# A fourth summed K pair in the gate projection of a SwiGLU block, and where its forms and the 512-column rows are kept

## The chip, the cores and the metric

The kernel runs on one core of a Trainium2 chip. The metric is the device time of one execution in microseconds (us). TensorE (PE) does the matmuls, VectorE (DVE) and ScalarE (ACT) prepare operands and move results, GpSimd (POOL) does a little, and the queue of SyncE (SP) starts nearly all transfers from memory.

## The reference

One layer of an encoder on 256 tokens of width 2048, all in float32: an attention part (latent attention beside differential attention), cross attention into 256 memory tokens, and a SwiGLU block of hidden width 5632, each added to the running x, then a last normalization. The change lies in the last block:

```python
hf = rms_norm(x, g_ffn[layer])
x = x + (jax.nn.silu(hf @ w_gate[layer]) * (hf @ w_up[layer])) @ w_down[layer]
return rms_norm(x, g_final)
```

## The kernel before, in words

**Products.** Each float32 operand is split in two parts: `h`, a rounded copy made by ACT (line 103), and `l`, what is left of it, made by DVE (line 104, a subtraction that needs the ACT copy). A product is three matmuls (`mm`, lines 95 to 97): h·h, h·l and l·h. A weight is read from memory into `wraw` (1 MB, three buffers), split into `wh`/`wl` tiles of 1024 columns (four buffers of each), and then used by PE. The activations stand still in PE, the weights move through it, 512 columns at a time.

**Chunks.** The hidden columns of SwiGLU are worked in one narrow chunk of 512 columns (`narrow_chunk`) and five wide chunks of 1024 columns (`wide_chunk`). There are three groups: the narrow chunk with the first wide one, then two wide chunks, then two wide chunks. After each group its hidden columns are multiplied with `w_down` (`wide_add`) into the running x. A wide chunk is a gate projection, Silu on its result, an up projection (both `wide_result`), the product of the two, and a transposition of that.

**K pairs.** In `wide_project` the 2048 input features are taken as eight pairs of 128-row blocks. A pair with 256 tokens and 1024 output columns is a 2x2 by 2x2 block product. There are two ways to do it, written as letters in `GU_KINDS` and `DN_KINDS`:

- `P`, plain: eight block products, that is 24 matmuls of 512 columns. Its weights are two `wh`/`wl` tiles of 1024 columns.
- `W`, summed: seven block products by a Strassen-Winograd scheme, that is 21 matmuls. DVE first makes sums of weight blocks in `tsum` (line 721 over 1024 columns, lines 725 and 726 over 512 each). The splits are then three tiles of 1024 columns (`b11`, `t13`, `t24`) and one of 512 (`b21`); `t24` lies in a place of its own, `wh2`/`wl2`, which has one buffer. Three of the products go straight into the accumulators `accs`, four into PSUM tiles `Q` that all summed pairs of a projection share.

When the last summed pair is done, `leave` (lines 751 to 755) combines the four Q on DVE; when the projection is done, `join` (line 759) adds the accumulators, four DVE instructions. The eight PSUM banks are two sets of four; accumulators and Q swap sets after every projection, and the transposes of the hidden columns (lines 327 and 850) use the same tiles as the next Q.

**The activations' forms.** `normalized_pairs` makes the stationary operands once, for gate and up together. A plain pair is a split of 512 columns. A summed pair (`summed_pair`) has eight forms, namely its four blocks and four sums of them (lines 684 to 687), then split. Pairs 2, 4 and 6 are summed. Plain pairs share two tiles of four K blocks; the fifth plain pair, number 7, has tiles `oddh`/`oddl` of its own in the pool `wsum`.

**Orders.** The gate takes the pairs in the order 0 to 7, whose kinds are P P W P W P W P. The up projection takes 0, 2, 1, 4, 3, 6, 5, 7, whose kinds are P W P W P W P P.

**What sets the order of work.** Only the transfers keep the written order. For all the rest a planner, which runs the program against its own timing of each instruction, lays down a fixed sequence for each engine ahead of the run. So PE does not take the matmuls pair by pair: where an operand of one pair is not yet there, matmuls of a neighbouring pair are put in between.

**Rows of 512.** `nat` gives tiles of 128 x 512 float32 with seven buffers in a pool that lives through the whole kernel. In SwiGLU they hold the sums of `summed_pair`, `sg` and `h` of the narrow chunk, and `v` and `u` of `wide_add`. The pools of attention are closed ahead of SwiGLU (line 646), and `wsum` is opened in their space (line 647).

Of the kernel before, what the change touches and what calls it, by code (L numbers as in the profile page):

```python
# [11 lines left out]
F32 = mybir.dt.float32  # L12
F32R = mybir.dt.float32r
# [6 lines left out]
P = 128  # L20
S = 256
# [14 lines left out]
NFC = FF // 512  # L36
NPC = (FF - 512) // 1024

GU_KINDS = "PPWPWPWP"

G_ORDER, U_ORDER = (0, 1, 2, 3, 4, 5, 6, 7), (0, 2, 1, 4, 3, 6, 5, 7)

DN_KINDS = "PP" + "PPPW" * NPC

# [32 lines left out]
def encoder_block(ctx: ExitStack, tc: tile.TileContext, a, out):  # L77
# [33 lines left out]
    def act_tile(shape=(P, 4, S), name="act"):  # L111
        return Split(
            act.tile(list(shape), F32R, name=name + "_h", tag="act"),
            act.tile(list(shape), F32R, name=name + "_l", tag="act"),
        )
# [37 lines left out]
    def project(actT, pieces, before=None, fine=0):  # L153
# [13 lines left out]
                kt += 1  # L167
        return accs

    def nat(name):  # L170
        return sb.tile([P, 512], F32, name=name, tag="nat", bufs=7)


    banks = [(pacc, "acc"), (pps, "ps")]
# [81 lines left out]
    for i in range(8):  # L256
# [10 lines left out]
        for k, w in enumerate(weights(a["w_in_lat"][i], i == 0, before_k=x0T.load_one if i == 0 else None,  # L267
                                      cut=QL if i == 0 else None, raw=lat_raw if i == 0 else None)):
            xk = x0T(2 * i + k)
            for tt in range(NT):  # L270
                x = xk[:, tt * P:(tt + 1) * P]
# [373 lines left out]
    soft_pool.close()  # L645
    attention.close()
    wsum = ctx.enter_context(tc.tile_pool(name="wsum", bufs=1))


    def pair_raw(src):  # L650
# [22 lines left out]
        def at(self, k, tt):  # L673
            return self.plain[:, k, tt * P:(tt + 1) * P] if self.forms is None else self.forms[:, 2 * tt + k, :]

    def summed_pair(a0, a1, in_psum=False):

        f = act_tile((P, 8, P), name="forms")
        s = nat("sums").rearrange("p (n t) -> p n t", n=4)
        a21 = a1[:, 0, :]  # L680
        if in_psum:
            a21 = nat("a21")[:, :P]
            nc.scalar.copy(out=a21, in_=a1[:, 0, :])
        nc.vector.tensor_tensor(out=s[:, 0, :], in0=a21, in1=a1[:, 1, :], op=ALU.subtract)
        nc.vector.tensor_tensor(out=s[:, 1, :], in0=a0[:, 0, :], in1=s[:, 0, :], op=ALU.subtract)
        nc.vector.tensor_tensor(out=s[:, 2, :], in0=a0[:, 0, :], in1=a21, op=ALU.subtract)
        nc.vector.tensor_tensor(out=s[:, 3, :], in0=a0[:, 1, :], in1=s[:, 1, :], op=ALU.subtract)
        split_into(f[:, 0:2, :], a0)
        split_into(f[:, 2:4, :], a1)
        split_into(f[:, 4:8, :], s)  # L690
        return Pair(forms=f)
# [97 lines left out]
    def normalized_pairs():  # L789

        rb = nat("rb")
        rps = ps_tile("rps")
        for tt in range(NT):
            nc.vector.tensor_copy(out=rb[:, tt * P:(tt + 1) * P], in_=rstdf[:, tt:tt + 1].to_broadcast([P, P]))
            nc.tensor.transpose(out=rps[:, tt * P:(tt + 1) * P], in_=rb[:, tt * P:(tt + 1) * P], identity=ident)
        rrow = nat("rrow")
        nc.scalar.copy(out=rrow[:, :S], in_=rps[:, :S])
        for xr in x2raw:
            nc.vector.tensor_tensor(out=xr, in0=xr, in1=rrow[:, :S].unsqueeze(1).to_broadcast([P, 4, S]), op=ALU.mult)
        pairs = []  # L800
        t, n = None, 4
        for i, kind in enumerate(GU_KINDS):
            xr = x2raw[i // 2][:, i % 2 * 2:i % 2 * 2 + 2, :]
            if kind == "P":
                if n == 4 and "P" in GU_KINDS[i + 1:]:
                    t, n = act_tile(name="x2n"), 0
                elif n == 4:
                    t = Split(*[wsum.tile([P, 2, S], F32R, name="odd" + x, tag="odd" + x, bufs=1) for x in "hl"])
                    n = 0
                split_into(t[:, n:n + 2, :], xr)  # L810
                pairs.append(Pair(t[:, n:n + 2, :]))
                n += 2
            else:
                pairs.append(summed_pair(xr[:, :, :P], xr[:, :, P:]))
        return pairs

    def narrow_chunk(c):
# [13 lines left out]

    def wide_chunk(c, spare):

        g = wide_result(xn, a["w_gate"][c], G_ORDER, GU_KINDS)
        for tt in range(NT):
            for oc in range(2):
                nc.scalar.activation(g[tt][:, oc, :], g[tt][:, oc, :], AF.Silu)
        u = wide_result(xn, a["w_up"][c], U_ORDER, GU_KINDS)
        t = act_tile(name="hT")
        pts = []  # L840
        for oc in range(2):
            for tt in range(NT):
                h = u[tt][:, oc, :]
                nc.vector.tensor_tensor(out=h, in0=h, in1=g[tt][:, oc, :], op=ALU.mult)
                if oc == 0:
                    transposed(t, h, tt, 4)
                    continue
                pt = ps_tile("pt")
                for j in range(4):
                    nc.tensor.transpose(out=pt[:, j * P:(j + 1) * P], in_=h[:, j * P:(j + 1) * P], identity=ident)  # L850
                pts.append(pt.rearrange("p (j t) -> p j t", t=P))
                split_into(spare[:, :, tt * P:(tt + 1) * P], pts[tt][:, 0:2, :])
        return [Pair(t[:, 0:2, :]), Pair(t[:, 2:4, :]), Pair(spare),
                summed_pair(pts[0][:, 2:4, :], pts[1][:, 2:4, :], True)]


    fss = small.tile([P, NT, 7], F32, name="fss", tag="fss", bufs=1)
# [103 lines left out]
def _lay_out(i):  # L961
# [32 lines left out]
        "w_xo": _pieces(i["w_xo"][0]),  # L994
        "w_gate0": _pieces(i["w_gate"][0][:, :512]),
        "w_up0": _pieces(i["w_up"][0][:, :512]),
        "w_gate": _pairs(i["w_gate"][0][:, 512:], GU_KINDS),
        "w_up": _pairs(i["w_up"][0][:, 512:], GU_KINDS),
        "w_dn": _pairs(i["w_down"][0], DN_KINDS),
        "w_down": _pieces(i["w_down"][0][-2048:, 1024:]).transpose(1, 0, 2, 3, 4),  # L1000
    }
# [18 lines left out]
```

## Time and profile before

| | |
|---|---|
| median of three runs | 1149.32 us (1148.9 to 1149.41) |
| the profiled execution's own time | 1149.22 us |
| its span, first to last instruction | 1147.4 us |
| granted TensorE clock over the span | 0.998 |
| SwiGLU's wide projections | about 480 us to 1054 us of the span |

Times in the trace are microseconds from the start of the span. "Busy" of an engine is time in which it executed something; the digits of the page are tenths of a slice of the span. In the list of groups a line reads: source line, engine, operation, tile written <- tiles read, shape, count, then busy time and the mean duration in ns, then the idle time of the engine just ahead and what ended it. In a timeline a line reads: start, duration, engine, line, operation, tiles, count, and in brackets the idle time ahead of it with what ended it. A duration can be longer than the distance between two starts, because neighbouring instructions of an engine overlap; the distance is what a queue of them costs.

### The profile page before, as it was taken

The numbers are of one execution on the slowest core, as the hardware profiler recorded it, in microseconds if no ns is written. First come the engines' busy times: TensorE is split into PE (matmuls) and PEld (weight loads), VectorE is DVE, ScalarE is ACT, GpSimd is POOL, SyncE is SP. The second block draws the span as 40 slices with busy tenths as digits, with TensorE's granted clock in tenths as the row PEclk, the third lists the DMA queues.
The fourth block names the chain that finished last, engine by engine and source line by source line (L and its number), as shares of the span: only waits on it lengthen the run. The fifth ranks groups of instructions, "written<-read, shape, count | busy, mean of one in ns | idle before, by whom it ended". The sixth has DMA issues, their size and how long they took to land.

```text
span 1147.4 us, 14386 instructions
## 1 busy us (share of the span) xinstructions
PE 1138.3 (99%) x5480; PEld 955.3 (83%) x5480; DVE 931.8 (81%) x1231; ACT 628.2 (55%) x885; POOL 68.9 (6%) x81
## 2 busy tenths in 40 slices
PE   9999999999999999999999999999999999999997
PEld 7888888888888888888888888888888888888887
DVE  7698766586868776989988889998888899898873
ACT  6755454554666555665544555564544564654552
POOL 5920000001000000000000000000000000000021
PEclk9999999999999999999999999999999999999999
DMA  9555334444764445455656555555555555565551
GB/s 359 217 211 187 126 130 169 176 150 182 294 214 158 166 159 182 153 214 187 217 183 220 184 190 214 183 205 198 188 215 187 210 190 205 195 233 210 191 212 75
DMA packets 33766, 222.15 MB, mean 194 GB/s; under 512 B 4128, under 2 KB 4896, under 8 KB 8992
## 3 DMA queue, kind: packets, MB, share of 16 engines
q1 hardware_dynamic: 32256, 216.86, 52.7%
q0 software_dynamic: 864, 3.15, 0.8%
q10 hardware_dynamic: 576, 1.21, 0.3%
q8 instruction: 43, 0.70, 0.2%
q14 instruction: 27, 0.22, 0.1%
HBM read 219.11 MB, written 2.10 MB: 193 GB/s over the span
## 4 chain that ended last, share of the span: by engine, by line
PE 98%; issue 0%; DMA 0%; DVE 0%; ACT 0%; POOLq 0%; POOL 0%; DVEq 0%; ACTq 0%
PE acc L95 27%; PE acc L96 27%; PE acc L97 27%; PE q L95 3%; PE q L97 3%; PE q L96 3%; PE pt L327 2%; PE ppt L474 1%; PE psc L97 1%; PE psc L96 1%; PE psc L95 1%; PE acckv L95 0%; PE acckv L97 0%; PE acckv L96 0%; PE pt L850 0%
## 5 line engine op out<-in xcount | busy, mean ns | idle before, releaser
L103 ACT CAST wh<-wraw 128x1024 fp32r<-128x1024 f32 (+2 forms) x399 | 395.3, 1003 | 368.6 <-PE acc L97 311.9
L104 DVE TENSOR_TENSOR wl<-wraw,wh 128x1024 fp32r<-128x1024 f32 (+2 forms) x399 | 464.2, 1175 | 142.6 <-ACT wh L103 140.6
L96 PE MATMUL acc<-wl,x2n_h 128*128 128x512 f32 x320 | 124.6, 390 | 0.0
L97 PE MATMUL acc<-wh,x2n_l 128*128 128x512 f32 x320 | 123.9, 389 | 0.0
L95 PE MATMUL acc<-wh,x2n_h 128*128 128x512 f32 x320 | 107.5, 390 | 0.0
L96 PE MATMUL acc<-wl,hT_h 128*128 128x512 f32 (+1 forms) x272 | 103.3, 381 | 0.0
L97 PE MATMUL acc<-wh,hT_l 128*128 128x512 f32 (+1 forms) x272 | 102.5, 380 | 0.0
L104 DVE TENSOR_TENSOR wl<-tsum,wh 128x1024 fp32r<-128x1024 f32 x76 | 91.9, 1220 | 8.6 <-ACT wh L103 8.5
L103 ACT CAST wh<-tsum 128x1024 fp32r<-128x1024 f32 x76 | 79.0, 1052 | 32.6 <-PE acc L97 11.9
L95 PE MATMUL acc<-wh,hT_h 128*128 128x512 f32 (+1 forms) x272 | 89.3, 381 | 0.0
L96 PE MATMUL acc<-wl,x0T_h 128*128 128x512 f32 x224 | 88.1, 394 | 0.1
L97 PE MATMUL acc<-wh,x0T_l 128*128 128x512 f32 x224 | 87.8, 393 | 0.0
L95 PE MATMUL acc<-wh,x0T_h 128*128 128x512 f32 x224 | 87.3, 395 | 0.4 <-ACT x0T_h L106 0.4
L97 PEld LDWEIGHTS acc<-wh,x2n_l 128*128 128x128 f32 x320 | 60.1, 188 | 12.4
L96 PEld LDWEIGHTS acc<-wl,x2n_h 128*128 128x128 f32 x320 | 60.1, 188 | 12.3
L95 PEld LDWEIGHTS acc<-wh,x2n_h 128*128 128x128 f32 x320 | 59.9, 188 | 12.3
L97 PEld LDWEIGHTS acc<-wh,hT_l 128*128 128x128 f32 x272 | 51.2, 188 | 9.6
L96 PE MATMUL q<-wl,forms_h 128*128 128x512 f32 x152 | 59.1, 389 | 0.0
L96 PEld LDWEIGHTS acc<-wl,hT_h 128*128 128x128 f32 x272 | 51.2, 188 | 9.5
L95 PEld LDWEIGHTS acc<-wh,hT_h 128*128 128x128 f32 x272 | 51.0, 188 | 9.5
L97 PE MATMUL q<-wh,forms_l 128*128 128x512 f32 x152 | 58.8, 389 | 0.0
L95 PE MATMUL q<-wh,forms_h 128*128 128x512 f32 x152 | 53.3, 389 | 0.0
(369 smaller groups left out, 2227.1 us busy)
## 6 DMA issues: line engine op xcount, KB each, us to landing
wraw<-in_w_gate SPq DMA_DIRECT2D x44, 1024.0 KB, 4.8
wraw<-in_w_up SPq DMA_DIRECT2D x44, 1024.0 KB, 4.8
wraw<-in_w_dn SPq DMA_DIRECT2D x36, 1024.0 KB, 4.8
wraw<-in_w_in SPq DMA_DIRECT2D x24, 1024.0 KB, 4.8
wraw<-in_w_out SPq DMA_DIRECT2D x16, 1024.0 KB, 4.8
wraw<-in_w_down SPq DMA_DIRECT2D x8, 1024.0 KB, 4.8
wraw<-in_w_in_lat SPq DMA_DIRECT2D x7, 832.0 KB, 7.4
wraw<-in_w_xk SPq DMA_DIRECT2D x4, 1024.0 KB, 6.3
```

Of the source, the lines that this page charges most:

```text
L95: nc.tensor.matmul(o, l.h, r.h, start=start, stop=False)
L96: nc.tensor.matmul(o, l.h, r.l, start=False, stop=False)
L97: nc.tensor.matmul(o, l.l, r.h, start=False, stop=stop)
L103: last_cast[0] = nc.scalar.copy(out=dst.h, in_=src).ins
L104: last_split[0] = nc.vector.tensor_tensor(out=dst.l, in0=src, in1=dst.h.bitcast(F32), op=ALU.subtract).ins
L327: nc.tensor.transpose(out=pt[:, j * P:(j + 1) * P], in_=src[:, j * P:(j + 1) * P], identity=ident)
L474: nc.tensor.transpose(out=pt[:, kt * S + tt * P:kt * S + (tt + 1) * P], in_=p[:, tt, kt * P:(kt + 1) * P], identity=ident)
```

## The change

The gate gets four summed pairs, numbers 1, 3, 5 and 7. The up projection keeps three, now 1, 3 and 5; its pair 7 is plain, and takes its four blocks out of the forms that the gate's pair 7 has. The gate's order is 0, 2, 1, 3, 4, 5, 7, 6, whose kinds are P P W W P W W P. The up projection's order is 0 to 7, whose kinds are P W P W P W P P, as before. The forms of pair 7 lie in `wsum` in place of `oddh`/`oddl`. The rows of 512 move: seven buffers in attention's pool, then five in `wsum`. The weights are laid out in memory ahead of the launch by the same letters (`_pairs`), each pair still 1 MB.

```diff
-GU_KINDS = "PPWPWPWP"
-
-G_ORDER, U_ORDER = (0, 1, 2, 3, 4, 5, 6, 7), (0, 2, 1, 4, 3, 6, 5, 7)
+G_KINDS, U_KINDS = "PWPWPWPW", "PWPWPWPP"
+
+G_ORDER, U_ORDER = (0, 2, 1, 3, 4, 5, 7, 6), (0, 1, 2, 3, 4, 5, 6, 7)
...
+    nat_pool = [early, 7]
+
     def nat(name):
-        return sb.tile([P, 512], F32, name=name, tag="nat", bufs=7)
+        pool, bufs = nat_pool
+        return pool.tile([P, 512], F32, name=name, tag="nat", bufs=bufs)
...
     wsum = ctx.enter_context(tc.tile_pool(name="wsum", bufs=1))
+    nat_pool[:] = wsum, 5
...
-    def summed_pair(a0, a1, in_psum=False):
-
-        f = act_tile((P, 8, P), name="forms")
+    def summed_pair(a0, a1, f=None, in_psum=False):
+
+        f = f or act_tile((P, 8, P), name="forms")
...
-        for i, kind in enumerate(GU_KINDS):
+        for i, kind in enumerate(G_KINDS):
             xr = x2raw[i // 2][:, i % 2 * 2:i % 2 * 2 + 2, :]
             if kind == "P":
-                if n == 4 and "P" in GU_KINDS[i + 1:]:
+                if n == 4:
                     t, n = act_tile(name="x2n"), 0
-                elif n == 4:
-                    t = Split(*[wsum.tile([P, 2, S], F32R, name="odd" + x, tag="odd" + x, bufs=1) for x in "hl"])
-                    n = 0
...
             else:
-                pairs.append(summed_pair(xr[:, :, :P], xr[:, :, P:]))
+                f = None
+                if i == 7:
+                    f = Split(*[wsum.tile([P, 8, P], F32R, name="forms" + x, tag="forms" + x, bufs=1) for x in "hl"])
+                pairs.append(summed_pair(xr[:, :, :P], xr[:, :, P:], f))
...
-        g = wide_result(xn, a["w_gate"][c], G_ORDER, GU_KINDS)
+        g = wide_result(xn, a["w_gate"][c], G_ORDER, G_KINDS)
...
-        u = wide_result(xn, a["w_up"][c], U_ORDER, GU_KINDS)
+        u = wide_result(xn, a["w_up"][c], U_ORDER, U_KINDS)
```

More of the change, by code (lines that the diff above doesn't have):

```diff
@@ L853, in wide_chunk @@
         return [Pair(t[:, 0:2, :]), Pair(t[:, 2:4, :]), Pair(spare),
-                summed_pair(pts[0][:, 2:4, :], pts[1][:, 2:4, :], True)]
+                summed_pair(pts[0][:, 2:4, :], pts[1][:, 2:4, :], in_psum=True)]
     fss = small.tile([P, NT, 7], F32, name="fss", tag="fss", bufs=1)
@@ L996, in _lay_out @@
         "w_up0": _pieces(i["w_up"][0][:, :512]),
-        "w_gate": _pairs(i["w_gate"][0][:, 512:], GU_KINDS),
-        "w_up": _pairs(i["w_up"][0][:, 512:], GU_KINDS),
+        "w_gate": _pairs(i["w_gate"][0][:, 512:], G_KINDS),
+        "w_up": _pairs(i["w_up"][0][:, 512:], U_KINDS),
         "w_dn": _pairs(i["w_down"][0], DN_KINDS),
```

## Prediction

> **What bounds the kernel now.** I read the page first: busy times, the slices, the chain.
>
> ```profile
> PE 1138.3 (99%) x5480; PEld 955.3 (83%) x5480; DVE 931.8 (81%) x1231; ACT 628.2 (55%) x885; POOL 68.9 (6%) x81
> DVE  7698766586868776989988889998888899898873
> PE 98%; issue 0%; DMA 0%; DVE 0%; ACT 0%; POOLq 0%; POOL 0%; DVEq 0%; ACTq 0%
> ```
>
> PE has work nearly all the time, and the chain that ended last is 98% PE. DVE is next: 81% over the span, but eights and nines from the seventeenth slice on, where SwiGLU begins. So PE sets the time, and the engine that feeds it has little left just where the change lies. The busy time by stage shows how little:
>
> ```profile
> 487.00:530.00 43.00, 43.00 (x193) 35.62 (x192) 38.56 (x43) 26.36 (x30) 0.00 (x0) 1.00 0.54 195
> 629.00:671.00 42.00, 42.00 (x187) 34.80 (x186) 35.99 (x40) 22.72 (x24) 0.00 (x0) 1.00 0.56 198
> 714.00:757.00 43.00, 43.00 (x199) 35.68 (x198) 39.86 (x50) 24.33 (x32) 0.00 (x0) 1.00 0.52 182
> 884.00:926.00 42.00, 42.00 (x187) 34.79 (x186) 35.59 (x38) 22.30 (x25) 0.00 (x0) 1.00 0.55 195
> 968.00:1011.00 43.00, 43.00 (x199) 35.72 (x198) 39.87 (x50) 24.38 (x31) 0.00 (x0) 1.00 0.50 180
> 1011.00:1054.00 43.00, 43.00 (x192) 35.60 (x191) 39.60 (x47) 23.94 (x28) 1.10 (x2) 1.00 0.64 236
> ```
>
> The columns after the stage are its length, then PE, PEld, DVE, ACT and POOL, the granted clock, the DMA share and GB/s. The first five rows are roughly the five gate projections. PE is busy without a gap in each, at clock 1.00. DVE is idle 4.44 us in the first (43.00 - 38.56), 6.01 in the second, 3.14 in the third, 6.41 in the fourth, 3.13 in the fifth. The second and fourth are the first chunk of a group and follow a down projection; the third and fifth are the second chunk and follow an up projection, whose joins, products and transposes fall into them.
>
> **What PE saves.** A summed pair in place of a plain one is 21 matmuls for 24. The price of one is the distance between starts:
>
> ```profile
> 729.35 0.39 PE L95 MATMUL acc<-wh,x2n_h 128*128 128x512 f32 x1
> 734.11 0.39 PE L97 MATMUL acc<-wh,x2n_l 128*128 128x512 f32 x1
> ```
>
> Between these two starts lie 21 steps of PE with no wait, so a matmul costs 4.76 / 21 = 0.2267 us; the 0.39 is a length, of which more than a third overlaps the next. Three fewer are 0.68 us, in five gates 3.40 us. This is the whole gain, if PE never waits. The up projection keeps three summed pairs in the same sequence of kinds, and its pair 7 is still 24 matmuls, so nothing changes there.
>
> **What DVE gets.** These are neighbours in DVE's queue, and the two splits by shape:
>
> ```profile
> 639.93 1.22 DVE L721 TENSOR_TENSOR tsum<-wraw 128x1024 f32<-128x1024 f32 x1
> 641.18 0.69 DVE L725 TENSOR_TENSOR tsum<-tsum,wraw 128x512 f32<-128x512 f32 x1
> 641.79 1.22 DVE L104 TENSOR_TENSOR wl<-wraw,wh 128x1024 fp32r<-128x1024 f32 x1
> 642.93 0.69 DVE L726 TENSOR_TENSOR tsum<-tsum,wraw 128x512 f32<-128x512 f32 x1
> 643.53 1.22 DVE L104 TENSOR_TENSOR wl<-wraw,wh 128x1024 fp32r<-128x1024 f32 x1
> L104 DVE TENSOR_TENSOR wl<-wraw,wh 128x1024 fp32r<-128x1024 f32 x344 | 420.3, 1233 | 115.6 <-ACT wh L103 113.8
> L104 DVE TENSOR_TENSOR wl<-wraw,wh 128x512 fp32r<-128x512 f32 x39 | 26.9, 691 | 20.4 <-ACT wh L103 20.1
> ```
>
> From 641.79 to 642.93 an instruction of 1024 columns took 1.14 us of the queue, from 642.93 to 643.53 one of 512 took 0.60. A plain pair has two splits of 1024: 2.28. A summed pair has three of 1024, one of 512, an add of 1024 and two of 512: 4 x 1.14 + 3 x 0.60 = 6.36. One more summed pair is 4.08 us more of DVE in each gate. Set against its matmuls, a plain pair leaves DVE a surplus of 24 x 0.2267 - 2.28 = 3.16 us, a summed pair a deficit of 6.36 - 4.76 = 1.60, and the new order has two summed pairs in a row, twice: 3.20 of deficit each time, which the plain pair between just repays. The gate shortens by 0.68, so a gate needs 4.08 + 0.68 = 4.76 us of DVE's idle time if PE is not to wait; what is missing is PE's waiting, which gives DVE the time back.
>
> The Trainium skill (VectorE: DVE Perf Modes, "The DRAIN you can't avoid") says that the next DVE instruction does not start until the pipeline is empty. The row at 643.53 disagrees: it starts 0.60 after one that is 0.69 long. By the page the full durations would count, and the added work would be 2 x 1.22 + 3 x 0.69 = 4.51 us, an estimate.
>
> **Once, in the first gate,** DVE also makes the forms of a fourth pair in place of the split of the fifth plain one:
>
> ```profile
> L104 DVE TENSOR_TENSOR forms_l<-sums,forms_h 128x512 fp32r<-128x512 f32 x8 | 5.4, 684 | 0.0
> L104 DVE TENSOR_TENSOR forms_l<-x2T_f,forms_h 128x256 fp32r<-128x256 f32 x6 | 2.3, 419 | 0.0
> L684 DVE TENSOR_TENSOR sums<-x2T_f 128x128 f32<-128x128 f32 x3 | 0.9, 284 | 0.0
> ```
>
> The split of the sums costs what the split of the plain pair did. Left are four sums and two splits of 256; less the overlap of 0.08 or 0.09 that the queue rows show, 4 x 0.20 + 2 x 0.34 = 1.48 us. DVE has no idle time just there, so it is paid out of the first gate's.
>
> **The sum.** The need is 4.76 us per gate, in the first 4.76 + 1.48 = 6.24. But a gate need not end even: DVE's lead over PE can be smaller at its end, and the up projection after it has idle time (43.00 - 39.60 = 3.40 in the sixth row). The four weight buffers hold at most two plain pairs, 10.88 us of PE. I let the lead take up what the deficit of one summed pair is, 1.60 us, since the up projection has more than that left to rebuild it. The second and fourth gates have 6.01 and 6.41: no wait. The third lacks 4.76 - 3.14 - 1.60 = 0.02, the fifth 0.03, the first 6.24 - 4.44 - 1.60 = 0.20. That is 0.25 us if all of DVE's idle time can be used. It can not quite be, because part of it is a full buffer and not want of work:
>
> ```profile
> 502.47 1.23 DVE L721 TENSOR_TENSOR tsum<-wraw 128x1024 f32<-128x1024 f32 x1 [0.21 <-DMA wraw<-in_w_gate]
> 513.69 1.23 DVE L104 TENSOR_TENSOR wl<-wraw,wh 128x1024 fp32r<-128x1024 f32 x1 [2.37 <-ACT wh L103]
> 515.49 1.23 DVE L104 TENSOR_TENSOR wl<-wraw,wh 128x1024 fp32r<-128x1024 f32 x1 [0.57 <-ACT wh L103]
> 730.68 1.23 DVE L104 TENSOR_TENSOR wl<-wraw,wh 128x1024 fp32r<-128x1024 f32 x1 [0.40 <-ACT wh L103]
> 736.80 3.50 DVE L104 TENSOR_TENSOR wl<-wraw,wh 128x1024 fp32r<-128x1024 f32 x3 [0.63 <-ACT wh L103]
> 745.67 0.69 DVE L104 TENSOR_TENSOR wl<-wraw,wh 128x512 fp32r<-128x512 f32 x1 [0.39 <-ACT wh L103]
> 747.00 1.23 DVE L104 TENSOR_TENSOR wl<-tsum,wh 128x1024 fp32r<-128x1024 f32 x1 [0.64 <-ACT wh L103]
> ```
>
> The wait at 730.68 lies ahead of the place where the second summed pair now comes, and what DVE could do then has no buffer. I take 0.25 of such lost time in each of the three tight gates, between 0 and the 0.40 of that row, nearer to the row. PE then waits 0.25 + 0.75 = 1.0 us in all, and the gain is 3.40 - 1.0 = 2.4 us. By the page's rule on the pipeline 0.43 more would be missing in each of the three, and the gain would be 1.1.
>
> **Costed at nothing.** ACT makes one more copy of 1024 and one of 512 per gate; it is busy 22 to 26 us of 42 to 43. The transfers are the same bytes, and two summed pairs in a row ask 1 MB per 4.76 us, some 220 GB/s, where the sixth row shows 236. The rows of 512: five buffers for what a group takes in turn (two per wide chunk, two per down half) come round only after another stage. Tight is only the narrow chunk, where the second `sg` would now reuse the second `sums`:
>
> ```profile
> 480.19 0.69 DVE L104 TENSOR_TENSOR forms_l<-sums,forms_h 128x512 fp32r<-128x512 f32 x1
> 481.45 1.29 DVE L104 TENSOR_TENSOR forms_l<-sums,forms_h 128x512 fp32r<-128x512 f32 x2
> 483.79 0.75 DVE L828 SCALAR_TENSOR_TENSOR h<-acc,x2Tr,sg 128x512 f32<-128x512 f32 x1
> ```
>
> If the first split in the pair at 481.45 is the second `sums`, it ends about 482.1, so `sg` (0.69) is there at 482.8, a microsecond before `h` needs it at 483.79. Without that cover the accumulators of the first gate would come free up to 1 us late, once.
>
> **Rivals.**
>
> *DVE's idle time is of no use where it lies.* Up to the fifth pair the gate has as many summed pairs as before, and the extra one comes seventh; then only the idle time late in a gate counts. In the third gate that is 1.66 of 3.14 (the rows at 736.80, 745.67 and 747.00), in the first 3.15 of 4.44 (the rows from 502.47 on). PE waits 4.76 - 1.66 = 3.10 in the third and (taken alike) the fifth, and 6.24 - 3.15 = 3.09 in the first, 9.29 in all; the lead of 1.60 takes 4.80 of it, and 4.49 - 3.40 = 1.1 us slower is left, within what counts as no change. Without the lead it is 5.9. For it: DVE is 93% busy in these stages. Against it: the planner puts matmuls of one pair among those of another, and so far PE never waits. Chance 0.30, at 1150.4 us, from 1147.0 to 1151.6 as the lead gives back more or less. In its extreme, DVE sets the pace of whole gates, and all five pay 4.08: 20.4 + 1.5 = 21.9 slower, 1171 us. The Trainium skill (Perfetto Trace Analysis, "Identifying the Most-Contended Engine") points there: matmul busy time is not the measure of PE, the busy share of weight loads is, and that is 83% against DVE's 93%. The trace speaks against it, since DVE's own waits in these rows end with ACT copies that wait for PE's buffers. Chance 0.02.
>
> *A wait for PSUM takes the place of the filler.* In the second chunk of a group two of the first summed pair's Q tiles are the banks of the last transposes, free only when the hidden columns' forms are split:
>
> ```profile
> 722.98 0.60 PE L850 MATMUL pt<-ident,res 128*128 128x128 f32 x4
> 734.88 0.68 DVE L104 TENSOR_TENSOR forms_l<-sums,forms_h 128x512 fp32r<-128x512 f32 x1
> 735.47 0.39 PE L95 MATMUL q<-wh,forms_h 128*128 128x512 f32 x1
> ```
>
> Meanwhile PE does the plain pair that follows, the 5.44 us from 729.35. Now a summed pair follows, of which only the twelve matmuls that need neither these banks nor `wh2` can run: 2.72 us. PE would wait the other 2.72, or, with DVE's 4.08 queued ahead of those splits, up to 6.80. No row is nearer to either; the middle is 4.76. In the two gates that is 9.5, less 3.4, plus 0.2 for the first: 6.3 us slower, 1155.6 us. At the low end it is 2.2 slower, 1151.6. It decides from (2.3 + 3.4 - 0.2) / 2 = 2.75 us a gate. Against it: DVE needs only some 2 us for these forms, and the transposes are done at 723.6, so the planner can draw them forward by several us. Chance 0.20.
>
> **The numbers.** About 0.2% (2.3 us) is what a measurement here can tell from no change. The forecast, 2.4 us of gain, has 0.48: faster. On the profiled execution it is 1149.22 - 2.4 = 1146.8, on the median 1149.32 - 2.4 = 1146.9. No change has 0.30, slower 0.20 + 0.02. The low end is the full 3.40 and the 0.4 that the runs spread: 1145.5. The high end takes in the first rival and the lower part of the second: 1153.0. The forecast's own range is 1145.5 to 1147.0.
>
> **What would show it.** Right: 15 matmuls fewer, PE's busy share still 99%, the five gates some 0.5 us shorter each, DVE above 95% in the third and fifth, and waits of PE for `wl` of about 1 us in all, after the second of two summed pairs. Wrong: PE idle before `q` ended by forms (the second rival), PE idle for `wl` of 3 us or more in the gates or the first pairs of the up projections (the first), or idle in the narrow chunk ended by `sg` or `h`.

## The result, and the profile after

The change makes the kernel slower: 1157.26 us median of six runs (1157.05 to 1158.17) against 1149.36 us (1148.9 to 1149.78) for the kernel before, a ratio of 1.0069 (95% interval 1.0058 to 1.0079), so 7.9 us. The prediction was 1146.9 us with a range of 1145.5 to 1153.0. The profiled execution took 1157.05 us with a span of 1155.3 us at a granted clock of 0.998, as before.

The page of the kernel after, its busy line, DVE's digits and the chain:

```profile
PE 1140.2 (99%) x5465; PEld 951.3 (82%) x5465; DVE 953.3 (83%) x1262; ACT 633.1 (55%) x897; POOL 67.6 (6%) x81
DVE  7688766586867776999988898999888998999873
PE 94%; DVE 3%; ACT 1%; issue 1%; DMA 0%; POOLq 0%; POOL 0%; DVEq 0%; ACTq 0%
```

The 15 matmuls are gone, PE is still shown 99% busy, and its busy time has grown. That is the trap of this page: a matmul that starts late is shown with a longer duration (0.50 us in the rows below where its neighbours have 0.39), and each duration overlaps the next start anyway. What tells is the chain, which now passes through DVE and ACT, and the distance between starts. The same five stretches of time as in the prediction (length, PE, PEld, DVE, ACT, POOL, clock, DMA share, GB/s); the work in them stands a few us later than before:

```profile
487.00:530.00 43.00, 42.31 (x186) 33.94 (x185) 40.73 (x46) 25.20 (x31) 0.00 (x0) 1.00 0.53 196
629.00:671.00 42.00, 42.00 (x187) 34.78 (x186) 38.54 (x42) 22.71 (x25) 0.00 (x0) 1.00 0.53 185
714.00:757.00 43.00, 41.56 (x187) 33.15 (x187) 41.02 (x53) 26.02 (x33) 0.00 (x0) 1.00 0.46 166
884.00:926.00 42.00, 42.00 (x187) 34.78 (x186) 38.53 (x41) 23.25 (x26) 0.00 (x0) 1.00 0.53 191
968.00:1011.00 43.00, 41.57 (x187) 33.15 (x187) 41.04 (x53) 24.24 (x32) 0.00 (x0) 1.00 0.44 150
```

In the third, 187 instructions of PE start where 199 did, and DVE still has 1.98 of its 3.14 us of idle time left (43.00 - 41.02): PE lost time while the idle time that was to prevent it lay unused. The same work ends 2.7 us later than before after the first group, 5.2 after the second, 7.8 after the third. Down projections add nothing.

Where PE loses it, from PE's timeline of the kernel after (start, duration, tiles, count, idle time ahead with its releaser):

```profile
471.87 0.61 PE L95 MATMUL acc<-wh,x2T_h 128*128 128x512 f32 x2
473.17 0.50 PE L95 MATMUL acc<-wh,x2n_h 128*128 128x512 f32 x1 [0.69 <-ACT wh L103]
...
676.93 0.39 PE L97 MATMUL q<-wh,forms_l 128*128 128x512 f32 x1
678.08 0.50 PE L95 MATMUL acc<-wh,forms_h 128*128 128x512 f32 x1 [0.76 <-ACT wh L103]
...
733.82 0.40 PE L97 MATMUL q<-wh,forms_l 128*128 128x512 f32 x1
734.71 0.50 PE L95 MATMUL acc<-wh,x2n_h 128*128 128x512 f32 x1 [0.49 <-ACT wh L103]
...
750.23 0.39 PE L97 MATMUL acc<-wh,forms_l 128*128 128x512 f32 x1
751.13 0.73 PE L95 MATMUL q<-wh,formsh 128*128 128x512 f32 x2 [0.51 <-ACT wh L103]
751.70 0.45 PE L95 MATMUL acc<-wh,formsh 128*128 128x512 f32 x1
752.59 0.50 PE L95 MATMUL acc<-wh,x2n_h 128*128 128x512 f32 x1 [0.45 <-ACT wh L103]
```

Every distance beyond 0.23 is lost. At 676.93, where the up projection begins after the second gate, it is 1.15 - 0.23 = 0.92, with small ones beside it 1.04. The places stand for: 1.4 us in the narrow chunk (once), 1.04 behind each gate that follows a down projection, about 0.8 and then 1.58 in each gate that follows an up projection; the first gate loses 1.2 at 500 and 515, with small ones 1.6. All such gaps from 430 to 1070 us, added up over the trace, are some 13 us against some 2 before. That is 10.6 to 11.1 more, by where the line is drawn for the smallest; less the 3.40 that the matmuls saved, it gives 7.2 to 7.7 of the 7.9.

Nearly all of these waits end with a copy of ACT, which the prediction costed at nothing. ACT is not short of time (633.1 us busy in 1155.3). Its copies wait in turn: over the whole span 46.1 us for DVE's sums in `tsum` (17.4 before), and otherwise mostly for a split buffer that PE still holds. At 676.93 it is a buffer, 1.19 us; in the kernel before, products of a plain pair stood in that place, and here PE has used them up.

What DVE does around the last of these, in DVE's timeline of the kernel after:

```profile
739.42 1.22 DVE L104 TENSOR_TENSOR wl<-wraw,wh 128x1024 fp32r<-128x1024 f32 x1 [1.11 <-ACT wh L103]
740.79 1.23 DVE L104 TENSOR_TENSOR wl<-tsum,wh 128x1024 fp32r<-128x1024 f32 x1
742.05 1.22 DVE L726 TENSOR_TENSOR tsum<-wraw 128x1024 f32<-128x1024 f32 x1
743.30 0.69 DVE L730 TENSOR_TENSOR tsum<-tsum,wraw 128x512 f32<-128x512 f32 x1
744.03 0.69 DVE L731 TENSOR_TENSOR tsum<-tsum,wraw 128x512 f32<-128x512 f32 x1
744.64 1.22 DVE L104 TENSOR_TENSOR wl<-tsum,wh 128x1024 fp32r<-128x1024 f32 x1
745.78 1.82 DVE L104 TENSOR_TENSOR wl<-wraw,wh 128x512 fp32r<-128x512 f32 x2
747.51 1.22 DVE L104 TENSOR_TENSOR wl<-tsum,wh 128x1024 fp32r<-128x1024 f32 x1
748.77 1.22 DVE L726 TENSOR_TENSOR tsum<-wraw 128x1024 f32<-128x1024 f32 x1
...
777.99 1.23 DVE L104 TENSOR_TENSOR wl<-tsum,wh 128x1024 fp32r<-128x1024 f32 x1 [0.52 <-ACT wh L103]
```

At 739.42 DVE has just waited 1.11 us for an ACT copy. That copy had waited for a free split buffer, until a product of PE gave one up, as ACT's timeline shows:

```profile
738.34 1.05 ACT L103 CAST wh<-wraw 128x1024 fp32r<-128x1024 f32 x1 [1.29 <-PE q L97]
```

From 739.42 to the wait ahead of 777.99 DVE waits for nothing, 38 us, and PE runs out at 750. One summed pair takes the queue from 742.05 to 748.77, 6.72 us, and not 6.36: an instruction that needs the one just ahead of it does not overlap with it. The add at 743.30 starts 1.25 after the sum that it reads, the next 0.73 after that; the split at 744.64, which needs neither of these two adds, 0.61 after. The sum at 748.77, which overwrites what the split ahead of it reads, starts 1.26 after it.

### The profile page after: what moved, and what is told of

Same layout as the page of the kernel before. It is cut to its first block, busy times and chain, and to the rows that moved or that the text cites. A ratio compares the mean times of both kernels' runs of the same rounds, so it can differ in the third digit from the quotient of the medians.

```text
span 1155.3 us, 14414 instructions
## 1 busy us (share of the span) xinstructions
PE 1140.2 (99%) x5465; PEld 951.3 (82%) x5465; DVE 953.3 (83%) x1262; ACT 633.1 (55%) x897; POOL 67.6 (6%) x81
## 4 chain that ended last, share of the span: by engine, by line
PE 94%; DVE 3%; ACT 1%; issue 1%; DMA 0%; POOLq 0%; POOL 0%; DVEq 0%; ACTq 0%
PE acc L95 25%; PE acc L96 25%; PE acc L97 25%; PE q L97 3%; PE q L96 3%; PE q L95 3%; PE pt L331 2%; DVE wl L104 1%; ACT wh L103 1%; PE ppt L478 1%; PE psc L97 1%; PE psc L96 1%; PE psc L95 1%; DVE tsum L726 1%; PE acckv L95 0%
## 5 line engine op out<-in xcount | busy, mean ns | idle before, releaser
L103 ACT CAST wh<-tsum 128x1024 fp32r<-128x1024 f32 x86 | 89.9, 1050 | 54.0 <-DVE tsum L726 24.6
L95 PE MATMUL acc<-wh,x2n_h 128*128 128x512 f32 x320 | 111.9, 393 | 3.2 <-ACT wh L103 3.2
L104 DVE TENSOR_TENSOR wl<-tsum,wh 128x1024 fp32r<-128x1024 f32 x86 | 104.5, 1219 | 8.6 <-ACT wh L103 8.3
L726 DVE TENSOR_TENSOR tsum<-wraw 128x1024 f32<-128x1024 f32 x43 | 52.4, 1218 | 2.0 <-DMA wraw<-in_w_dn 1.0
```

Of the source, the lines that this page charges most:

```text
L95: nc.tensor.matmul(o, l.h, r.h, start=start, stop=False)
L103: last_cast[0] = nc.scalar.copy(out=dst.h, in_=src).ins
L104: last_split[0] = nc.vector.tensor_tensor(out=dst.l, in0=src, in1=dst.h.bitcast(F32), op=ALU.subtract).ins
L726: nc.vector.tensor_tensor(out=t[:, 0:2, :], in0=raw[:, 1:3, :], in1=raw[:, 0:1, :].to_broadcast([P, 2, 512]), op=ALU.add)
```

## The experiments

The theory after the result: DVE's idle time before the added work can not be drawn on, because it ends when a buffer comes free; only what lies behind it could, and there is too little (the first rival, without its lead). Against it stood a cost in the new rows or forms, a cost of the neighbouring summed pairs as such (PSUM, the second rival), the plain amount of DVE's work, and ACT's copies, with which most of PE's waits end.

### Which part of the change costs

**Rows alone**: the kernel before, with the rows of 512 as in the change.

```diff
+    nat_pool = [early, 7]
...
-        return sb.tile([P, 512], F32, name=name, tag="nat", bufs=7)
+        pool, bufs = nat_pool
+        return pool.tile([P, 512], F32, name=name, tag="nat", bufs=bufs)
...
+    nat_pool[:] = wsum, 5
```

> The kernel before with only the rows of 512 moved (seven in attention's space, then five in SwiGLU's). Theory, VectorE is late with the weights' splits in the gates: nothing of it is here, so 1149.4 us within 0.5. Rival, the moved rows make a wait (the narrow chunk of the changed kernel loses 1.4 us near 472): about 1150.8 us, with a gap on TensorE near 472.

Measured: 1149.48 us against 1149.62, ratio 1.0 (0.999 to 1.0009). The rows cost nothing.

**Gate without additions**: the kernel after, whose gate splits raw blocks in place of sums.

```diff
+            if kinds is G_KINDS:
+                t = raw[:, 0:4, :]
...
+            if kinds is not G_KINDS:
                 nc.vector.tensor_tensor(out=t[:, 2, :], in0=t[:, 0, :], in1=raw[:, 2, :], op=ALU.add)
...
```

> The changed kernel, but the gate's summed pairs leave out the three additions of weight blocks: the splits read the raw blocks in place of the sums. VectorE has 4 x 2.34 = 9.4 us less in each gate. Theory, VectorE's time is what TensorE waits for: the gaps in the gates go, 13.2 - 2.3 = 10.9 us of them less the 1.4 in the narrow chunk; about 1147.5 us. Rival, the wait for PSUM in the second chunk of a group: its 0.8 us stays in each of the two and the rest goes, 1149. Rival, the fixed cost of two summed pairs in a row (buffers, not VectorE's time): over 1153 us.

Measured: 1149.66 us, ratio 1.0 (0.9991 to 1.0009). 7.6 us come back. ACT makes as many copies as before (485) and is busy 637.0 us against 633.1, so ACT's work as such is not the cost. The run takes out more of DVE's work than the change put in, 9.4 us a gate against 4.08; it shows that DVE's additions are needed for nearly all of the loss, not that their amount alone makes it. And 1147.5 was missed by 2: the second and third group gain 0.80 and 0.72 of their 1.36, and the first still loses 2.05, in the narrow chunk and at 483. That pointed to the forms.

**Last pair without additions**: the same in the gate's last summed pair alone (`bare = kinds is G_KINDS and i == summed[-1]`).

> The changed kernel, but the last summed pair of each gate leaves out its three additions (the splits read the raw blocks in place of the sums): 2.34 us less of VectorE per gate, a quarter of what the run without any additions left out. Theory, VectorE's time is short by what the change gave it: since the need is about 4 us a gate and this is more than half of it, about half of the 7.6 us that all additions gave comes back, 1153.5 us. Rival, a fixed cost of two summed pairs in a row: 1156 us or over.

Measured: 1153.5 us against 1149.55, ratio 1.003 (1.0019 to 1.0041), as expected. 2.34 us less of DVE per gate, 11.7 in all, are worth 3.8 us.

**Forms alone**: rows moved and the forms of pair 7 made, but used as a plain pair in both projections.

```diff
-                    t = Split(*[wsum.tile([P, 2, S], F32R, name="odd" + x, tag="odd" + x, bufs=1) for x in "hl"])
-                    n = 0
+                    f = Split(*[wsum.tile([P, 8, P], F32R, name="forms" + x, tag="forms" + x, bufs=1) for x in "hl"])
+                    pairs.append(summed_pair(xr[:, :, :P], xr[:, :, P:], f))
+                    continue
```

> The kernel before with the rows moved and with pair 7's eight forms made in the narrow chunk in place of its plain split; the gate and the up projection then both take pair 7 as plain, out of its forms. Matmuls and weights' splits are those of before. Theory, the making of the forms is paid in the narrow chunk and the first gate, where VectorE has no idle time: TensorE loses there what it lost in the run without additions, 2.05 + 0.68 = 2.7 us; about 1152.2 us. Rival, the forms are hidden and that loss comes from the summed pairs: 1149.5 us.

Measured: 1152.08 us against 1149.29, ratio 1.0022 (1.0012 to 1.0031). In the trace, whose execution took 1151.25 us, 2.02 us are lost, all in the narrow chunk. PE's timeline of this kernel:

```profile
471.63 0.61 PE L95 MATMUL acc<-wh,x2T_h 128*128 128x512 f32 x2
472.94 0.50 PE L95 MATMUL acc<-wh,x2n_h 128*128 128x512 f32 x1 [0.69 <-ACT wh L103]
474.27 0.50 PE L96 MATMUL acc<-wl,x2T_h 128*128 128x512 f32 x1 [0.83 <-DVE wl L104]
```

PE waits for weights of the narrow chunk, whose splits stand in DVE's queue behind the forms.

**Late forms**: the kernel after, with these forms made once the narrow chunk's up projection is written.

```diff
+    def last_pair():
+        xr = x2raw[3][:, 2:4, :]
+        f = Split(*[wsum.tile([P, 8, P], F32R, name="forms" + x, tag="forms" + x, bufs=1) for x in "hl"])
+        return summed_pair(xr[:, :, :P], xr[:, :, P:], f)
...
+        xn.append(last_pair())
```

> The changed kernel with pair 7's forms written in the program after the narrow chunk's up projection, so that the planner has the weights' splits ahead of them. Theory, the forms stood ahead of splits that TensorE waited for near 472: most of the 2.2 us there goes, about 1155.3 us. Rival, VectorE has no idle time until the first gate wherever the forms stand: 1157.3 us, the gaps only moved.

Measured: 1156.53 us, ratio 1.0062 (1.0047 to 1.0077). That lies between the two expectations. The gap of 1.4 in the narrow chunk is gone, but the first gate loses some 0.6 more than in the kernel after, at 500 and 516; its group is still 2.29 late, 0.58 of which stands already ahead of SwiGLU.

### Place or amount

**Additions twice, last pair**: the kernel before; the three additions of the gate's last summed pair are made twice, 1.14 + 2 x 0.60 = 2.34 us more of DVE per gate, no buffer, matmul or transfer touched.

```diff
+            again = 2 if src.tensor.name == "in_w_gate" and i == summed[-1] else 1
+            for _ in range(again):
...
```

> The kernel before, with the three additions of the gate's last summed pair made twice: 2.34 us more of VectorE per gate, the same matmuls, splits, buffers and order. VectorE's idle time in the five gates was 3.13 to 6.41 us. The prediction's step, idle time of a gate can be used: 1149.4 us within 0.5. Theory now, much of that idle time lies where the buffers are full and is no use to a later pair: the two second chunks and the first gate lose 1 to 2 us each, 1152 to 1155 us.

Measured: 1155.57 us against 1149.55, ratio 1.0049 (1.0034 to 1.0064): 6.0 of the 11.7 us added are lost, though each gate had 3.1 us or more of idle time; that is a little over the 1152 to 1155 expected. The loss is not spread evenly. By the starts of PE's matmuls the three groups lose 1.4, 2.2 and 2.6 us, all in or behind the first, third and fifth gate. The second and fourth lose nothing, though their last pair was doubled too. DVE's waits in the second gate show why, first in the kernel before, then with the doubled additions:

```profile
659.72 0.69 DVE L104 TENSOR_TENSOR wl<-wraw,wh 128x512 fp32r<-128x512 f32 x1 [1.07 <-ACT wh L103]
662.37 1.23 DVE L104 TENSOR_TENSOR wl<-wraw,wh 128x1024 fp32r<-128x1024 f32 x1 [1.95 <-ACT wh L103]
```

```profile
663.57 1.23 DVE L104 TENSOR_TENSOR wl<-wraw,wh 128x1024 fp32r<-128x1024 f32 x1 [0.38 <-ACT wh L103]
665.17 2.36 DVE L104 TENSOR_TENSOR wl<-wraw,wh 128x1024 fp32r<-128x1024 f32 x2 [0.37 <-ACT wh L103]
```

Behind the last pair's first sum this gate had 3.40 us of waits in the kernel before (these two rows and two of 0.2), and 1.19 are left (these two and one of 0.44): 2.2 of the 2.34 us went into waits that stood behind the added work. The fourth gate has the same rows. In the third gate only 1.03 stood behind it (the rows at 745.67 and 747.00 in the prediction). The first gate fits less well: 2.94 stood behind, 1.05 are left, and 1.4 us are lost all the same.

**Additions twice, first pair**: the same with `summed[0]`.

> The kernel before, with the three additions made twice at the gate's first summed pair instead of its last: the same 2.34 us more of VectorE per gate as in the run that cost 6.0 us, but ahead of the waits of VectorE in the gate instead of behind them. Theory, idle time of VectorE can pay only for work that stands before it: the waits at the second and third summed pair now take it up, 1149.5 to 1151 us. Rival, VectorE's amount in the gate decides wherever it stands: 1155.5 us again.

Measured: 1149.9 us against 1149.61, ratio 1.0002 (0.9992 to 1.0011). The same 2.34 us, two summed pairs earlier, cost nothing: the profiled execution is 0.54 us longer than that of the kernel before, and 0.53 of that stands already at 93 us, far ahead of SwiGLU. The third gate, first with the last pair's additions doubled, then with the first pair's:

```profile
714.00:757.00 43.00, 43.00 (x199) 35.71 (x198) 39.76 (x50) 23.68 (x31) 0.00 (x0) 1.00 0.48 175
```

```profile
714.00:757.00 43.00, 43.00 (x199) 35.70 (x198) 41.97 (x55) 24.13 (x32) 0.00 (x0) 1.00 0.50 183
```

3.24 us of idle time remain in the first case (43.00 - 39.76), 1.03 in the second. DVE's and PE's timeline with the last pair's doubled:

```profile
731.84 1.23 DVE L104 TENSOR_TENSOR wl<-wraw,wh 128x1024 fp32r<-128x1024 f32 x1 [0.41 <-ACT wh L103]
734.56 1.23 DVE L104 TENSOR_TENSOR wl<-tsum,wh 128x1024 fp32r<-128x1024 f32 x1 [0.97 <-ACT wh L103]
737.96 3.50 DVE L104 TENSOR_TENSOR wl<-wraw,wh 128x1024 fp32r<-128x1024 f32 x3 [0.63 <-ACT wh L103]
...
756.26 1.23 DVE L723 TENSOR_TENSOR tsum<-wraw 128x1024 f32<-128x1024 f32 x1 [1.08 <-DMA wraw<-in_w_up]
```

```profile
759.98 0.46 PE L95 MATMUL q<-wh,forms_h 128*128 128x512 f32 x1
761.67 0.50 PE L96 MATMUL q<-wl,forms_h 128*128 128x512 f32 x1 [1.23 <-DVE wl L104]
```

The waits at 731 to 738, ahead of the doubled additions, stay. Behind them DVE is late. The next load needs a `wraw` buffer that the doubled additions still read; it starts at 750.70 and lands at 756.16, where in the kernel before it started at 746.39. DVE waits 1.08 us for it while PE's stock runs down: 1.69 - 0.23 = 1.46 us are lost at 759.98. So for the same amount of work, its place decides what it costs: it is free only where enough waits stand behind it.

### Neighbours and PSUM

**Three in a row**: the kernel before with the gate's kinds P P W W P P W P, three summed pairs as before, two of them neighbours.

```diff
-G_ORDER, U_ORDER = (0, 1, 2, 3, 4, 5, 6, 7), (0, 2, 1, 4, 3, 6, 5, 7)
+G_ORDER, U_ORDER = (0, 1, 2, 4, 3, 5, 6, 7), (0, 2, 1, 4, 3, 6, 5, 7)
```

> The kernel before with the gate's order 0 1 2 4 3 5 6 7, kinds P P W W P P W P: three summed pairs as before, two of them now in a row once. Theory, VectorE's total decides: 1149.4 us within 0.7. Rival, two in a row decide: each of the five gates loses about 1 us at that place, 1153 to 1155 us.

Measured: 1152.4 us, ratio 1.0024 (1.0014 to 1.0033), between the two expectations: not five gates lose, but two. The second and third group lose 0.95 each. Its PE timeline in the third gate:

```profile
731.06 0.40 PE L97 MATMUL q<-wh,forms_l 128*128 128x512 f32 x1
731.93 0.73 PE L95 MATMUL acc<-wh,x2n_h 128*128 128x512 f32 x2 [0.47 <-ACT wh L103]
```

This is the gap at 733.82 of the kernel after: a summed pair in the place of the plain pair that had filled the wait for PSUM. The copy that PE waits for here had itself waited 0.50 us for a split buffer, and the products into Q go on only at 734.69, behind DVE's last read of the transposes (733.80). That PSUM is the reason is read from this order; no run frees the banks earlier.

**One neighbour**: the kernel after, kinds P W P W P W W P (`G_ORDER` = 0, 1, 2, 3, 4, 5, 7, 6).

> The changed kernel with the gate's order 0 1 2 3 4 5 7 6, kinds P W P W P W W P: four summed pairs, but only one place with two in a row. Theory, VectorE's total in a gate decides: the additions are the same, so 1155 to 1158 us. Rival, the two in a row decide (a deficit of 3.2 us at a stroke instead of 1.6): half the loss in the gates goes, about 1152.5 us.

Measured: 1156.38 us, ratio 1.0058 (1.0041 to 1.0074). The later groups lose 1.54 and 1.6 in place of 2.57, the first 4.05 in place of 2.69. Without the first two neighbours, the waits at 676.93 and 733.82 of the kernel after are gone; the last two still lose 1.9 in each gate that follows an up projection. In the first group PE also waits in the narrow chunk, 0.80 us ended by `sg` at 482.60 and 0.44 by `h` at 485.57. That is a sign of being wrong that the prediction had named, but the rows as such are not shown to be the reason: on ACT `sg` stands behind a copy that had waited 0.62 us for a buffer.

**Pairs early**: the kernel after, kinds P W W P W P W P (`G_ORDER` = 0, 1, 3, 2, 5, 4, 7, 6), so that the extra additions lie ahead of DVE's idle time.

> The changed kernel with the gate's order 0 1 3 2 5 4 7 6, kinds P W W P W P W P: the same four summed pairs, the two in a row now at the beginning of the gate, ahead of VectorE's waits, and the end of the gate as in the kernel before. Theory, extra work of VectorE is free ahead of its waits: the loss late in the gates and at the start of the up projections goes, the forms' 2 us and a wait for the first summed pairs' operands stay, 1149 to 1152 us. Rival, two in a row or the amount cost the same anywhere: 1156 to 1158 us.

Measured: 1156.23 us against 1150.26, ratio 1.0055 (1.004 to 1.007). So the expected 1149 to 1152 us was missed. The gates that follow a down projection lose nothing any more. The two later groups still lose 2.1 and 2.2 us, in the gates that follow an up projection, from 727 to 742, and the first has the waits for `sg` and `h` again, 0.80 and 0.42. DVE's timeline of this kernel:

```profile
732.97 0.69 DVE L104 TENSOR_TENSOR forms_l<-sums,forms_h 128x512 fp32r<-128x512 f32 x1
735.84 1.22 DVE L104 TENSOR_TENSOR wl<-wraw,wh 128x1024 fp32r<-128x1024 f32 x1 [2.18 <-ACT wh L103]
```

DVE stands idle 2.18 us, for a copy that had waited 1.82 us until a product of PE into Q gave a buffer up. PE loses 0.79 behind it, at 736.20, and 0.60 at 741.45, for copies of ACT; the 0.97 ahead of it, at 729.13, ends with a split of DVE. So the extra additions here stand ahead of a wait that they can not shorten, since the buffers are held by products that need the banks of the last transposes. That is the second rival's mechanism, as far as the order of the rows shows it; its share is not told apart from DVE's.

**Pairs early, late forms**: both.

> The same order with pair 7's forms written after the narrow chunk's up projection, where the gaps of the narrow chunk went away before and came back in the first gate. Theory: with the end of the first gate eased they need not come back, 0.5 to 2 us less than the run with the order alone. Rival: VectorE has no idle time in the first gate anyway, the same time as the order alone within 0.5.

Measured: 1155.97 us, ratio 1.005 (1.0033 to 1.0066), 0.3 less than with the order alone, as the rival had it.

### Ways out of DVE's queue

**Additions on GpSimd**: the kernel after, the gate's two additions of 512 there (`eng = nc.gpsimd if kinds is G_KINDS else nc.vector`).

> The changed kernel with the gate's two additions of 512 columns on GpSimd, which is idle there; an addition of 512 takes it 1.92 us by the rows of the kernel before, against 0.60 of VectorE's queue. VectorE has 4 x 1.20 = 4.8 us less in each gate, a little more than the change gave it. Theory, VectorE's time is what TensorE waits for: the loss of the second and third group, 2 x 2.57, turns into most of a gain, about 1152 us with the narrow chunk's loss left. Rival, the longer way from the raw weights to the split (3.8 us on GpSimd) or a shared port costs as much: 1156 us or over.

Measured: 1165.97 us, ratio 1.0143 (1.0128 to 1.0158), 8.7 slower than the kernel after, as the rival had it. Its two reasons, the longer way and the slower splits, are not told apart. Groups of this kernel, then the same split in the kernel after:

```profile
L732 POOL TENSOR_TENSOR tsum<-tsum,wraw 128x512 f32<-128x512 f32 x20 | 36.7, 1834 | 1.6
L104 DVE TENSOR_TENSOR wl<-wraw,wh 128x512 fp32r<-128x512 f32 x44 | 41.8, 949 | 16.0 <-ACT wh L103 15.8
```

```profile
L104 DVE TENSOR_TENSOR wl<-wraw,wh 128x512 fp32r<-128x512 f32 x44 | 30.2, 686 | 17.4 <-ACT wh L103 17.4
```

**Sums in two tiles**: the kernel after, with `tsum` as two tiles `ta` and `tb`, so that a sum needs not wait for the split of the last `t24`.

```diff
-            t = wsum.tile([P, 4, 512], F32, name="tsum", tag="tsum", bufs=1)
+            ta = wsum.tile([P, 2, 512], F32, name="ta", tag="ta", bufs=1)
+            tb = wsum.tile([P, 2, 512], F32, name="tb", tag="tb", bufs=1)
```

> The changed kernel with the sums of the weights in two tiles of 1024 columns, one buffer each, instead of one tile of 2048: the next pair's first addition then need not wait for the split of this pair's last two sums. No VectorE work changes. Theory, VectorE's time decides: 1157.3 within 1. Rival, VectorE idles because the one buffer of sums is held: 1154 us or less.

Measured: 1160.78 us, ratio 1.01 (1.0083 to 1.0117), 3.5 slower than the kernel after. Its list of DVE's waits (total, times, longest) shows why:

```profile
DVE ta L727 <- DMA wraw<-in_w_up: 6.4, 8, 2.9
DVE ta L727 <- DMA wraw<-in_w_gate: 2.7, 6, 0.9
```

The planner put the sums earlier in DVE's fixed sequence, where they wait for their weights with everything behind them; in the kernel after, such waits for the gate's and up projection's weights are 0.8 us in all. Whether the one buffer of sums costs anything stays open.

**A fifth split buffer**, paid with two tiles of activations, in the kernel after and in the kernel with the rows alone:

```diff
-    act = ctx.enter_context(tc.tile_pool(name="act", bufs=24))
+    act = ctx.enter_context(tc.tile_pool(name="act", bufs=22))
...
-        pool, tags, bufs = (wp, ("wh", "wl"), 4) if pool is None else (pool, ("wh2", "wl2"), 1)
+        pool, tags, bufs = (wp, ("wh", "wl"), 5) if pool is None else (pool, ("wh2", "wl2"), 1)
```

> The changed kernel with five buffers of split weights in place of four (the space is taken from the activations' tiles, 22 in place of 24). No engine's work changes; VectorE and ScalarE can be one split further ahead. Theory, idle time that ends with a full buffer is what is lost: it becomes usable and the loss in the gates falls by 2 us or more, 1155 us or less. Rival, VectorE has no time to be ahead with: 1157.3 us within 0.7.

> The control for the fifth buffer: the kernel before with the rows moved, five buffers of split weights and 22 activation tiles. TensorE has no gaps in the kernel before, so both theories expect 1149.4 us within 0.5; anything more is the price of the two activation tiles.

Measured: 1171.14 us, ratio 1.0186 (1.0171 to 1.0201), and 1157.52 us, ratio 1.0071 (1.0055 to 1.0088). The second lost its 7.5 us wholly in attention, where the two tiles are missing; the first lost 14.0 us in SwiGLU. A fifth buffer shows no gain, but what the two tiles do in SwiGLU is not told apart: inconclusive.

### Where four summed pairs pay

**First chunks alone**: the kernel after, four summed pairs only in the gates that follow a down projection, three in the others.

```diff
-        g = wide_result(xn, a["w_gate"][c], G_ORDER, G_KINDS)
+        four = c in (1, 3)
+        g = wide_result(xn, a["w_gate"][c], G_ORDER if four else G3_ORDER, G_KINDS if four else U_KINDS)
...
```

> The changed kernel with four summed pairs only in the gates of the second and fourth wide chunk, which follow a down projection and where VectorE was idle 6.0 and 6.4 us; the other three gates have three, in the old sequence of kinds, with pair 7 plain out of its forms. The prediction's step, no wait in these two gates: the forms' 2.0 us (by the trace of the run with the forms only) less 2 x 0.68, so 1150.2 us. Theory now, each of the two loses about 1.0 us at the start of the up projection that follows: 1152 us. Rival, the loss of the changed kernel is spread over all gates alike: 1152 + 1.5 = 1153.5 us or over.

Measured: 1152.05 us against 1149.61, ratio 1.002 (1.001 to 1.0029). Gaps of 1.04 and 1.03 behind the two gates, 1.4 in the narrow chunk. The prediction had these gates at no wait, with 6 us of idle time each. Behind the last pair's first sum, the second gate had 3.40 us of it, against the need of 4.76.

**First chunks, pairs early, late forms**: as the last, with `G_ORDER` = 0, 1, 3, 2, 5, 4, 7, 6 in these two gates and the forms made late.

> Four summed pairs only in the gates of the second and fourth wide chunk, there in the early order 0 1 3 2 5 4 7 6 (in the run with that order these two gates and their up projections had no gaps); the other gates have three; pair 7's forms are written after the narrow chunk's up projection. Theory, every bit of VectorE's added work now stands ahead of idle time: two gates save 0.68 each, and the first gate with three summed pairs has 4.4 us idle for the forms, so 1149.6 - 1.4 = 1148.2 us, 1150 if the forms are not hidden. Rival, the forms cost their 2 us wherever they stand: 1150.3 us or over.

Measured: 1148.45 us against 1149.58, ratio 0.9987 (0.9978 to 0.9996). PE has only the gaps of the kernel before, and the two later groups end 0.68 us earlier each. The second gate:

```profile
629.00:671.00 42.00, 42.00 (x187) 34.75 (x187) 39.91 (x44) 24.15 (x26) 0.00 (x0) 1.00 0.57 201
```

DVE works 39.91 us where it worked 35.99, and PE does not wait: with the work ahead of the idle time, it is used. The run is 0.13% faster than the kernel before (0.04 to 0.22), close to the 1148.2 us that were expected.

## Why the prediction was wrong, point by point

- **What PE saves: right.** 0.68 us a gate, seen where nothing waits, in the last experiment.
- **What DVE gets: nearly right.** DVE's busy time grew by 953.3 - 931.8 = 21.5 us, against 5 x 4.08 + 1.48 = 21.9. In the queue a summed pair takes 6.72, 0.36 more than 6.36, since three of its seven instructions need the one ahead of them. The prediction's own rows had it: 639.93 to 641.18 is 1.25, not 1.14. The Trainium skill (VectorE: DVE Perf Modes, "The DRAIN you can't avoid") says that the next instruction waits for an empty pipeline, and adds that one that is not held starts earlier. The rows agree with the addition: 0.61 from start to start for a duration of 0.69 where the next does not need the one ahead. Where it does, it is 1.25 for 1.22; no run here shows whether the Trainium skill means that by "held". The prediction read only the row at 643.53 and did not use 1.25.
- **The sum: this step failed.** It set the need of a gate against all of DVE's idle time there and took 1.60 us of lead besides, with 0.25 per tight gate for time that could not be used. Idle time ends with a split buffer coming free: DVE is then as far ahead as it can be, and what is unused is gone. Only waits behind the added work can shrink. The doubled additions showed it: 6.0 us for work at the last summed pair, 0.3 (no measurable change) for the same work at the first; and at the last pair itself nothing in the gates with 3.40 us of waits behind it, some 2.2 us in the third with 1.03. There the lead gave nothing back. The 0.25 rested on the wait of 0.40 at 730.68; the longest wait of that gate, in the kernel before, is not among the prediction's rows and lies ahead of the added pair as well (below). "The second and fourth gates: no wait" fell with it: the wait of 1.04 comes at the start of the up projection behind them.

```profile
733.40 1.23 DVE L104 TENSOR_TENSOR wl<-tsum,wh 128x1024 fp32r<-128x1024 f32 x1 [0.97 <-ACT wh L103]
```

- **The forms: mis-placed, 1.48 taken as covered by the first gate.** They cost 2.0 us in the narrow chunk, whose splits stand behind them in the queue; made later, they cost about 0.7 us less, and what is left of their cost shows in the first gate, where four summed pairs left little room.
- **Rows of 512, ACT, transfers: right** for the rows. ACT's copies end most of PE's waits, but without DVE's additions the same copies are nearly all in time. The transfers are hidden as long as DVE is in time; DVE's lateness delays them in turn.
- **The first rival** had the mechanism. Without its lead it gave 5.9 us slower; its 1.1 with the lead, the value that it was priced at, was the error. It gave 3.10 us of waiting to the third gate, where about 2.4 was measured, and nothing to the second and fourth, where 1.04 was. Its extreme, 21.9 us, to which the Trainium skill (Perfetto Trace Analysis, "Identifying the Most-Contended Engine") pointed, had the direction; 7.9 was measured, because part of DVE's idle time was used.
- **The second rival** exists at about 0.95 us in each gate that follows an up projection, as three in a row showed, and not at its 4.76. Where the pairs are drawn forward it may be more; that was not told apart.

Of the 7.9 us, 3.4 are gained with the matmuls, 2.0 go to the forms, some 1.9 to the neighbours, and the rest, 7.4, is put down to additions that come too late in a gate. This rest is a difference, not a measurement, and the parts are not independent. Since the planner lays down a new sequence for every edit, differences of a microsecond between variants can be order and not mechanism; this was not told apart. Nor was a fifth split buffer tried without taking its space from elsewhere.

## What to carry to other kernels

Don't add up the idle time of a feeding engine: list its waits in order and count only those that stand behind the added work, since a wait for a full buffer ahead of it can not be saved up. Doubling a harmless instruction at two places of a stage measures this with few lines. When the busy share of PE says 99%, look at the distances between starts before you believe it.

## What was not expected of the hardware

An addition of 512 columns in float32 took GpSimd 1.50 and 1.83 us as the profile shows it (1503 ns in the group of the first, 1834 in that of the second; spans of this engine are rough), against 0.69 on DVE. With these additions on GpSimd, DVE's splits of 512 columns took 0.949 us on average in place of 0.686. The average hides two kinds: 11 of the 44, each beside an addition on GpSimd, took 1.67 to 1.78 us, the others at most 0.69 as before, among them two that stood beside one for 0.6 us. The Trainium skill (GPSIMD Engine Reference, Key points) says that the two engines share their way to the on-chip memory and that a DVE instruction with two inputs there contends for it, as these splits have. The rows agree: the joins of 512 columns, which read one of their inputs from PSUM, took 0.68 us beside an addition on GpSimd as without it. Moving two of DVE's instructions per summed pair to an idle engine thus slowed some of those that stayed. And DVE's instructions overlap by some 0.08 us only where the second doesn't need the first.
